# An expert layer's gate matrix with its tokens in pairs, and more of the up products placed beside the routing

## The chip, the cores and the metric

The kernel runs on one NeuronCore of a Trainium2 chip. One launch computes a stack of three model blocks for 256 tokens of width 1024. The metric is the device time of a launch in microseconds (us), as the median of several executions. A profiled execution of the same program gives the busy times, waits and clocks that are quoted here.

The engines are called PE (matrix products; PEld is its loading of the stationary operand), DVE (vector), ACT (scalar and activation), POOL (GpSimd) and SP (which here only issues DMAs). ACT also issues DMAs; both do it in the order of their own queue.

## The reference, cut to what matters

Three blocks follow each other. Only the last layer of the first one is touched by the change. It is a layer of 16384 single-neuron experts: for each token 8 heads pick 16 experts each, through the best sums of two sub-key scores.

```python
def peer_ffn(h, w_q, sub_k1, sub_k2, expert_u, expert_v):
    q = (ht @ w_q).reshape(T, PEER_HEADS, PEER_QDIM)
    s1 = jnp.einsum('thd,nd->thn', q[..., :PEER_HALF], sub_k1)
    s2 = jnp.einsum('thd,nd->thn', q[..., PEER_HALF:], sub_k2)
    v1, i1 = lax.top_k(s1, PEER_TOPK)
    v2, i2 = lax.top_k(s2, PEER_TOPK)
    cand = (v1[..., :, None] + v2[..., None, :]).reshape(T, PEER_HEADS, PEER_TOPK * PEER_TOPK)
    cand_idx = (i1[..., :, None] * PEER_NKEYS + i2[..., None, :]).reshape(...)
    vals, pos = lax.top_k(cand, PEER_TOPK)
    experts = jnp.take_along_axis(cand_idx, pos, axis=-1)
    gates = jax.nn.softmax(vals, axis=-1)
    ...
    u = expert_u[ec]                      # [c, heads, 16, D] of the picked experts
    a = jnp.einsum('cd,chkd->chk', xc, u)
    w = jax.nn.gelu(a) * gc
    return jnp.einsum('chk,chkd->cd', w, expert_v[ec])
```

Here T = 256 tokens, 128 keys on each side, 16 of the best on each side and 16 of the best sums.

## The kernel before

**Streams and products.** All weights come from device memory in chunks of 1 MB, `[128, 2048]` float32. `stream` (line 89) loads a chunk through SP's DMA queue into one of 3 raw buffers and splits it in two halves: ACT casts the high part (L99), and DVE or, if `pool` is set, POOL subtracts it to get the low part (L101). The split parts have 3 buffers in this layer. A float32 product is then three products of the parts (`mm3`, L117 to L119). An *up chunk* holds the up weights of 256 experts; its two halves make 2 x 8 x 3 = 48 matmuls of 256 columns.

**The layer.** The kernel doesn't gather experts. It computes every expert's up product with every token, multiplies it by a dense gate matrix that is zero for experts that were not picked, and multiplies the result by every expert's down weights. There are 64 up chunks and 64 down chunks.

- `routing` (line 791) makes the gate matrix in 48 steps. Steps 0 to 3: query projection, scores against the keys (L804) and the top 16 of both sides on DVE. Steps 4 to 9 and 10 to 15, for the two token tiles: top 16 of the sums, the picked positions back to key indices (L859 to L865, on DVE), and three transposes on PE (L867 twice, L871), so that the indices `iT` and the gates `gT` (high and low float16 parts) lie with the picks on partitions and the tokens along the row. Steps 16 to 47: eight tokens a step. DVE compares the 8 tokens' indices with all 128 keys, which gives the one-hot tiles E (L888) and B (L889), and multiplies E by the two parts of the gates to get A (L892, two instructions). For each token two matmuls (L897) of B and A sum over the picks and give its 128 x 128 gates. ACT takes them out of PSUM, 4 tokens at a time (L900), and after every 16 tokens a 1 MB tile `gt` goes to the device array `gd` (L902).
- `up` (line 904) yields after each up chunk: stream, two products, and GELU on ACT (L912) into a tile `ga`.
- `down` (line 916) runs over the 64 down chunks. Every four chunks it reads 1 MB of gates back (`G`, L936, on ACT's queue). Each chunk multiplies its two `ga` tiles by the gates on DVE (L945), splits them (L112 on ACT, L113 on DVE) and makes 24 matmuls of 512 columns (L928, L929, L931) into four accumulators.

**What sets the order.** `weave` (line 339) emits, after step i of `routing`, n(i) steps of `up`: none before step 7, one a step from 7 to 19, then two of five steps, 24 in all. The first down step emits 5 more up chunks, and each later one emits one, until all 64 are done. The 58 `ga` tiles, one for each half chunk, hold 29 chunks. POOL does the subtractions of the first 29 up chunks, DVE those of the later ones and of all down chunks. Each engine works its queue in order. The tile framework orders the queues by the order of emission, where an engine's operands are ready by its own reckoning, and puts in the waits. The one-hot tiles have 8 buffers, which is two steps of B, E and two A.

In a one-hot tile `[128, 128, 8]` the token is the innermost index, so the 128 columns of one token, which PE reads for L897 as stationary and as moving operand, are 8 float16 apart.

Of the kernel before, what the change touches and what calls it, by code (L numbers as in the profile page):

```python
# [7 lines left out]
F32 = mybir.dt.float32  # L8
# [18 lines left out]
class Core:  # L27
    """Pools and the pieces that every block uses.

    Weights stream through SBUF in chunks of [128, 2048]; each float32 chunk is split  # L30
    exactly into a part with 12 significant bits and the rest, and a float32 product is
    hi*hi + hi*lo + lo*hi, accumulated in float32.
    """
# [18 lines left out]
    def ring(self, ctx, n):  # L52
        """Buffers of the weight stream, n of the split parts."""
        self.raw = ctx.enter_context(self.tc.tile_pool(name="raw", bufs=3))
        self.slots, self.turn, self.early = [], 0, []
        self.more(ctx, n)

    def more(self, ctx, n):
        """n more buffers of the split parts while ctx is open."""
        pool = ctx.enter_context(self.tc.tile_pool(name=f"split{len(self.slots)}", bufs=n))  # L60
        self.slots += [pool] * n

        def less():
            del self.slots[-n:]
        ctx.callback(less)

    def work(self, ctx, half_rows=1):
        """Buffers of the norms: rows of gains, a token tile's rows."""
# [3 lines left out]
    def temp(self, ctx, name):  # L72
        """Buffers of one part of the kernel."""
# [47 lines left out]
    def row(self, name, n=D, src=None, pool=None, tag=None, p=128):  # L121
        """A row of a parameter on every partition."""
# [5 lines left out]
    def rsqrt_n(self, ss, n, m, p=128):  # L128
        """(ss / n + EPS) ** -0.5 for [p, m]."""
# [7 lines left out]
    def rstd(self, parts, n, p=128):  # L137
        """Reciprocal root mean square of rows of n that come in one or two parts [p, m <= 512]."""
# [17 lines left out]
    def pre_norm(self, t, g):  # L156
        """xh, xl[:, :, t] = split(transpose(rmsnorm(X[t]) * g))"""
# [10 lines left out]
    def put_off(self, f, *args):  # L168
        """Emits f(*args), now or at the next flush."""
# [10 lines left out]
    def post_norm(self, t, acc, g, scale, gn=None):  # L180
        """X[t] += scale * rmsnorm(acc) * g, and the next part's pre_norm if it has gains gn."""
# [10 lines left out]
    def residual(self, t, acc, gn):  # L192
        """X[t] += acc, and the next part's pre_norm."""
# [5 lines left out]
    def to_T(self, xn, hi, lo, t, nb, kb0=0, scale=None):  # L199
        """hi, lo[:, kb0.., t] = split(transpose(xn) * scale), scale a power of two."""  # L200
# [15 lines left out]
    def cols_steps(self, w, done):  # L216
        """w: [groups, 2, 128, 4 * N], N <= 512 output columns a group; done(j, t, psum).
        The first two groups go one token tile at a time, as the tiles get ready, if the ring has room."""
# [24 lines left out]
    def linear_stat(self, hl, i, ps):  # L243
        """ps [128, n] = 128 output features by tokens; hl: a chunk [128, 2, 8, 128], i: which half."""
# [5 lines left out]
    def lead(self, ch, done):  # L250
        """Products of the chunks ch one token tile at a time, as the tiles get ready, with the tokens as
        rows; done(c, t, psum [128, 2, 128])."""
# [9 lines left out]
    def pair(self, hl, between=lambda: None):  # L262
        """The two products of a chunk."""
# [6 lines left out]
    def stat_pairs(self, chunk, n, lead=0, row=None):  # L270
        """The two products of each of n chunks. The first chunks go one token tile at a time, with the
        tokens as rows [128, 256] in row(c, t), and are then transposed."""
# [30 lines left out]
    def linear_rows(self, w, hi, lo, done, tail=3, pool=0):  # L303
        """w: [K / 256, 128, 2048] rows in pairs of blocks; hi, lo: [128, K / 128, S]."""
# [34 lines left out]
def weave(main, side, n):  # L339
    """Emits the steps of main, and n[i] steps of side after step i."""  # L340
# [5 lines left out]
def head_norm(k, pool, ps, nh, gain, tag, p=128):  # L346
    """Per-head rmsnorm of ps [p, nh * 64]; returns [p, nh, 64] in SBUF."""
# [13 lines left out]
def rope(k, pool, q, nh, cs, sn, p=128):  # L361
    """Rotary embedding of the first 16 dims of q [p, nh, 64], in place; cs, sn: [p, 16]."""
# [10 lines left out]
def attend(k, pool, p, q, segs, v, identb, sink=None):  # L373
    """Masked attention of p queries and 8 heads.

    q(h): [64, p]; segs(h): (keys [64, n], n, additive mask [p, n] or None) for each piece of the
    keys; v(s, h): [n, 64]. Returns psum [p, 8, 64] before the division, and the factors [p, 8].
    """
# [65 lines left out]
def gelu_small(k, pool, out, x, n, p):  # L444
    """tanh form of gelu for small SBUF tiles, in the table of exp."""
# [10 lines left out]
class Block1:  # L456
# [108 lines left out]
    def compress(self):  # L565
        """The compressed keys and values; yields where the tensor engine would wait."""
# [59 lines left out]
    def cmp_scores(self, t):  # L626
        """Exponentials of the compressed keys' scores [128, 8, 15] and their factors [128, 8]."""
# [21 lines left out]
    def cmp_out(self, s):  # L649
        """psum [128, 8, 64]: the exponentials' products with the compressed values."""  # L650
# [12 lines left out]
    def attention(self, t):  # L663
# [10 lines left out]
        def add(b, o, r, first=False):  # L674
            """y = or += the gated output of branch b"""
# [20 lines left out]
    def flush(self, keep=0):  # L696
        """Emits the transposes that were put off, but for the last."""
# [3 lines left out]
    def merge(self):  # L701
        k, nc, pool = self.k, self.k.nc, self.pool
        M = [k.xn() for t in range(2)]
        for h in range(2):
            ch = [k.stream(k.a["w_up_" + n][h, 0]) for n in "ab"]
            for t in range(2):
                ts = slice(t * 128, t * 128 + 128)
                c = slice(h * 512, h * 512 + 512)
                for i, n in enumerate("ab"):
# [6 lines left out]
                    # sigmoid(z) = (1 + tanh(z / 2)) / 2; the half is in to_T  # L716
# [38 lines left out]
class Peer:  # L755
    """Every expert's product with every token; a gate matrix, zero where the expert was not
    retrieved, weighs them. The gates come from the top-k of the sub-keys' scores; as two float16 parts
    of SCALE times them they keep float32's 24 bits."""

    AHEAD = 58  # L760
# [3 lines left out]
    def __init__(self, k, pool):  # L764
        self.k, self.pool = k, pool
        self.ga = {}
        self.gd = k.dram.tile([128, S // self.GRP, 128, self.GRP], F32, name="gd")

    def consts(self):
        k = self.k  # L770
        tl = lambda n, sh, dt=F32: self.rp.tile(sh, dt, name=n)
        self.iota = tl("iota", [128, 128, 8], F16)
        k.nc.gpsimd.iota(self.iota, pattern=[[1, 128], [0, 8]], base=0, channel_multiplier=0,
# [17 lines left out]
    def routing(self):  # L791
# [21 lines left out]
        for t in range(2):  # L813
# [40 lines left out]
            for j in range(2):  # L854
# [5 lines left out]
                                        self.iota[:, 0:16, None, :].to_broadcast([128, 16, 16, 8]), op=OP.is_equal)  # L860
# [950 lines left out]
```

## Time and profile before

| | us |
|---|---|
| median of 3 runs | 3044.96 |
| lowest and highest of them | 3044.13, 3054.55 |
| the profiled execution, from its first to its last instruction | 3048.1 |
| PE busy in it | 2919.3 |
| the expert layer's steps 4 to 15, with up products | 364 to 463.7 |
| one-hot steps, with up products | 463.7 to 683.3 |
| down chunks with an up chunk each | about 700 to 1090 |
| down chunks alone | about 1090 to 1240 |

How to read what follows. The page of the profile gives each engine's busy time and share of the span, and rows of 40 equal slices (76.2 us each), in which a digit is tenths; PEclk is the clock that PE was granted, in tenths of full speed. A row of the groups names line, engine, operation, tile and shape, then the busy time and the mean duration in ns, then the idle time before them with what ended it. A row of the stages gives the window and its length, the busy time of each engine with its number of instructions, the granted clock, the share of the DMA engines and the GB/s. A row of the waits says who waited for whom: us in total, times, longest. A row of the timeline gives start and duration in us. Matmuls overlap, and their ends are modelled, so starts say more than durations.

### The profile page before, as it was taken

Reading aid. Unit: us, or ns where it says so; the run is one execution under the profiler, and the core shown is the slowest. Engines: PE = TensorE matmul, PEld = TensorE weight load, DVE = VectorE, ACT = ScalarE, POOL = GpSimd, SP = SyncE. Lnnn points to the kernel's source line nnn. Section 1 sums busy time; section 2 is a strip of 40 time slices with the busy share of each in tenths; the row PEclk is TensorE's granted clock in tenths of the full one; section 3 lists DMA queues with packets and bytes.
Section 4 is the critical chain, followed back from the end, with each engine's and each line's share of the span. In section 5 each row is a group of like instructions: output and inputs, shape, how many; then the busy total and the mean of one; then the engine's idle time right before and its main releaser. Section 6 shows DMA issues by size and latency. Waiting matters only on the chain. (4 is left out here: it accounts for less than half of the span.)

```text
span 3048.1 us, 44684 instructions
## 1 busy us (share of the span) xinstructions
PE 2919.3 (96%) x18182; PEld 2586.9 (85%) x18182; DVE 1773.9 (58%) x2984; ACT 1367.2 (45%) x2318; POOL 421.3 (14%) x337
## 2 busy tenths in 40 slices
PE   8999979999999999999679999999999989999999
PEld 6787978889999988898669989898997878878897
DVE  6645693437555555655966555476655555455654
ACT  4533433335444555544535444343544444444543
POOL 2000663221000000000650000032001010000100
PEclk9968988789999999999889999999999899998999
DMA  5512433339766555554325555543554424443453
GB/s 211 187 56 85 153 124 130 134 137 324 251 205 211 206 193 193 205 187 169 131 69 182 185 194 181 192 156 116 175 182 153 145 87 166 152 139 111 145 187 111
DMA packets 105982, 496.74 MB, mean 163 GB/s; under 512 B 11040, under 2 KB 44320, under 8 KB 50224
## 3 DMA queue, kind: packets, MB, share of 16 engines
q1 hardware_dynamic: 61632, 443.15, 42.1%
q10 hardware_dynamic: 44144, 50.74, 5.0%
q8 instruction: 142, 2.33, 0.3%
q14 instruction: 64, 0.52, 0.1%
HBM read 476.03 MB, written 17.83 MB: 162 GB/s over the span
## 5 line engine op out<-in xcount | busy, mean ns | idle before, releaser
L101 DVE TENSOR_TENSOR wl<-raw,wh 128x1024 fp32r<-128x1024 f32 x764 | 915.4, 1219 | 617.7 <-ACT wh L99 616.4
L99 ACT CAST wh<-raw 128x1024 fp32r<-128x1024 f32 x848 | 861.3, 1041 | 708.2 <-PE acc L118 220.5
L117 PE MATMUL tp<-xx,wh 128*128 128x256 f32 (+1 forms) x1440 | 424.2, 295 | 5.6 <-ACT ga L912 5.6
L119 PE MATMUL acc<-xx,wl 128*128 128x256 f32 x1504 | 425.1, 283 | 2.2 <-POOL wl L101 1.4
L117 PE MATMUL acc<-xx,wh 128*128 128x256 f32 x1504 | 424.6, 282 | 2.4 <-DVE hp L1093 2.4
L118 PE MATMUL acc<-xx,wh 128*128 128x256 f32 x1504 | 425.5, 283 | 0.0
L118 PE MATMUL tp<-xx,wh 128*128 128x256 f32 (+1 forms) x1440 | 421.8, 293 | 0.0
L119 PE MATMUL tp<-xx,wl 128*128 128x256 f32 (+1 forms) x1440 | 420.6, 292 | 0.8 <-POOL wl L101 0.8
L117 PEld LDWEIGHTS tp<-xx,wh 128*128 128x128 f32 x1440 | 286.7, 199 | 10.5 <-ACT ga L912 6.0
L118 PEld LDWEIGHTS tp<-xx,wh 128*128 128x128 f32 x1440 | 287.1, 199 | 3.7
L119 PEld LDWEIGHTS acc<-xx,wl 128*128 128x128 f32 x1504 | 286.9, 191 | 2.6 <-POOL wl L101 1.6
L117 PEld LDWEIGHTS acc<-xx,wh 128*128 128x128 f32 x1504 | 286.6, 191 | 2.6 <-issue 2.6
L119 PEld LDWEIGHTS tp<-xx,wl 128*128 128x128 f32 x1440 | 286.4, 199 | 1.8 <-POOL wl L101 1.0
L118 PEld LDWEIGHTS acc<-xx,wh 128*128 128x128 f32 x1504 | 284.7, 189 | 0.0
L147 POOL TENSOR_SCALAR va<-ss 128x1 f32<-128x1 f32 (+1 forms) x49 | 26.0, 531 | 1810.3 <-ACT junk L143 1628.8
L101 POOL TENSOR_TENSOR wl<-raw,wh 128x1024 fp32r<-128x1024 f32 x84 | 219.5, 2630 | 232.8 <-ACT wh L99 221.3
L117 PE MATMUL acc<-wh,xx 128*128 128x256 f32 (+2 forms) x672 | 223.3, 334 | 3.2 <-ACT xx L112 3.2
L118 PE MATMUL acc<-wl,xx 128*128 128x256 f32 (+2 forms) x672 | 219.7, 328 | 4.2 <-DVE wl L101 4.2
L119 PE MATMUL acc<-wh,xx 128*128 128x256 f32 (+2 forms) x672 | 218.7, 328 | 1.2 <-DVE xx L113 1.2
L928 PE MATMUL o<-wh,wth 128*128 128x512 f32 x512 | 200.6, 392 | 0.0
L929 PE MATMUL o<-wl,wth 128*128 128x512 f32 x512 | 200.1, 391 | 0.0
L931 PE MATMUL o<-wh,wtl 128*128 128x512 f32 x512 | 159.9, 391 | 0.0
(480 smaller groups left out, 5113.2 us busy)
## 6 DMA issues: line engine op xcount, KB each, us to landing
raw<-in_ffn_in_dram SPq DMA_DIRECT2D x88, 1024.0 KB, 4.9
raw<-in_peer_u_dram SPq DMA_DIRECT2D x64, 1024.0 KB, 4.9
raw<-in_peer_v_dram SPq DMA_DIRECT2D x64, 1024.0 KB, 4.9
raw<-in_ffn_out_dram SPq DMA_DIRECT2D x44, 1024.0 KB, 4.9
raw<-in_w_up_dram SPq DMA_DIRECT2D x32, 1024.0 KB, 4.9
raw<-in_w_down_dram SPq DMA_DIRECT2D x32, 1024.0 KB, 4.9
gd<-gt ACTq DMA_DIRECT2D x16, 1024.0 KB, 4.0
G<-gd ACTq DMA_DIRECT2D x16, 1024.0 KB, 7.0
```

The lines of the kernel that those rows point to most:

```text
L99: nc.scalar.copy(h[:, c], r[:, c])
L101: eng.tensor_tensor(l[:, c], r[:, c], h[:, c].bitcast(F32), op=OP.subtract)
L117: mm(out, ah, bh, start=start, stop=False)
L118: mm(out, ah, bl, start=False, stop=False)
L119: mm(out, al, bh, start=False, stop=stop)
L147: nc.gpsimd.tensor_scalar(v, ss[:, 0:1], EPS, ss[:, 1:2], op0=OP.add, op1=OP.add)
L928: mm(acc[t][h], wh, vh[:, h], start=st, stop=False)
L929: mm(acc[t][h], wh, vl[:, h], start=False, stop=False)
L931: mm(acc[t][h], wl, vh[:, h], start=False, stop=sp)
```

## The change

It has two parts.

In the one-hot tiles the 8 tokens of a step are laid out as 4 pairs: `[128, 4, 128, 2]`, pair, key, token of the pair. The 128 columns of a token are then 2 float16 apart. The compared table of key numbers is made in that layout, with two columns a key (`iota2`), and the older table keeps only the 16 rows that the index step uses.

The up products are kept by whole chunks in 29 tiles of `[128, 2, 256]`, as much memory as before. During routing 40 chunks are meant to be emitted instead of 24: n(i) is two or one in steps 7 to 19 and then two of three steps. All 40 are split on POOL. Chunks 0 to 21 keep their tile. Chunks 22 to 39 (18 of them) are written to a device array `gs` by a DMA on ACT's queue, and give their tile back. `down` fetches them again, also on ACT's queue, whenever fewer than 27 chunks are held after a chunk was used.

```diff
-    AHEAD = 58
+    SLOTS = 29
+    KEPT = 22
+    AHEAD = 40
...
+        self.held, self.spilled = 0, []
+        self.gs = k.dram.tile([128, self.AHEAD - self.KEPT, 2, S], F32, name="gs")
...
-        self.iota = tl("iota", [128, 128, 8], F16)
-        k.nc.gpsimd.iota(self.iota, pattern=[[1, 128], [0, 8]], base=0, channel_multiplier=0,
+        self.iota = tl("iota", [128, 16, 8], F16)
+        k.nc.gpsimd.iota(self.iota, pattern=[[1, 16], [0, 8]], base=0, channel_multiplier=0,
+                         allow_small_or_imprecise_dtypes=True)
+        self.iota2 = tl("iota2", [128, 128, 2], F16)
+        k.nc.gpsimd.iota(self.iota2, pattern=[[1, 128], [0, 2]], base=0, channel_multiplier=0,
...
-                    oh = lambda n_: pool.tile([128, 128, 8], F16, tag="oh", name=n_, bufs=8)
+                    oh = lambda n_: pool.tile([128, 4, 128, 2], F16, tag="oh", name=n_, bufs=8)
                     B, E = oh("B"), oh("E")
-                    bc = lambda x: x[:, None, c].to_broadcast([128, 128, 8])
-                    nc.vector.tensor_tensor(E, bc(self.iT[0]), self.iota, op=OP.is_equal)
-                    nc.vector.tensor_tensor(B, bc(self.iT[1]), self.iota, op=OP.is_equal)
+                    bc = lambda x: x[:, c].rearrange("p (a b) -> p a b", b=2)[:, :, None].to_broadcast([128, 4, 128, 2])
+                    iota = self.iota2[:, None].to_broadcast([128, 4, 128, 2])
+                    nc.vector.tensor_tensor(E, bc(self.iT[0]), iota, op=OP.is_equal)
+                    nc.vector.tensor_tensor(B, bc(self.iT[1]), iota, op=OP.is_equal)
...
-                                nc.tensor.matmul(ps[:, i, :], B[:, :, z * 4 + i], A[j][:, :, z * 4 + i],
+                                nc.tensor.matmul(ps[:, i, :], B[:, z * 2 + i // 2, :, i % 2], A[j][:, z * 2 + i // 2, :, i % 2],
...
-            hl = k.stream(k.a["peer_u"][c], pool=c < self.AHEAD // 2)
+            hl = k.stream(k.a["peer_u"][c], pool=c < self.AHEAD)
+            g = self.slot()
             for i in range(2):
                 ps = k.tp((128, S), tag="tq")
                 k.linear_stat(hl, i, ps)
-                g = self.pool.tile([128, S], F32, tag="ga", name="ga", bufs=self.AHEAD)
-                nc.scalar.activation(g, ps, AF.Gelu_apprx_tanh)
-                self.ga[c * 2 + i] = g
+                nc.scalar.activation(g[:, i], ps, AF.Gelu_apprx_tanh)
+            if self.KEPT <= c < self.AHEAD:
+                nc.scalar.dma_start(self.gs[:, c - self.KEPT], g)
+                self.spilled.append(c)
+            else:
+                self.ga[c] = g
+                self.held += 1
             yield
+    def slot(self):
+        return self.pool.tile([128, 2, S], F32, tag="ga", name="ga", bufs=self.SLOTS)
+    def fetch(self):
+        while self.spilled and self.held < self.SLOTS - 2:
+            c = self.spilled.pop(0)
+            self.ga[c] = self.slot()
+            self.held += 1
+            self.k.nc.scalar.dma_start(self.ga[c], self.gs[:, c - self.KEPT])
...
-                w = self.ga.pop(e)
+                w = self.ga[c][:, i]
...
+            del self.ga[c]
+            self.held -= 1
+            self.fetch()
...
-            x = i >= 7 if i < 20 else i % 5 in (0, 3)
-            x = min(x, self.AHEAD // 2 - 5 - done[0])
+            x = 0 if i < 7 else 1 + i % 2 if i < 20 else i % 3 > 0
+            x = min(x, self.AHEAD - done[0])
```

The rest of the diff empties lines that held comments.

More of the change, by code (lines that the diff above doesn't have):

```diff
@@ L859, in routing @@
                 nc.vector.tensor_tensor(eq, sel[j].rearrange("p (k h) -> p k h", h=8)[:, None].to_broadcast([128, 16, 16, 8]),
-                                        self.iota[:, 0:16, None, :].to_broadcast([128, 16, 16, 8]), op=OP.is_equal)
+                                        self.iota[:, :, None, :].to_broadcast([128, 16, 16, 8]), op=OP.is_equal)
                 nc.vector.tensor_tensor(eq, eq, ib[:, :, None, :].to_broadcast([128, 16, 16, 8]), op=OP.mult)
```

## The prediction

> **What bounds the kernel now.** I read the page first, then the busy times by stage, and inside the routing stage the groups, the instruction timeline and the waits. The page gives the size of the whole and says which engine to watch.
>
> ```profile
> span 3048.1 us, 44684 instructions
> PE 2919.3 (96%) x18182; PEld 2586.9 (85%) x18182; DVE 1773.9 (58%) x2984; ACT 1367.2 (45%) x2318; POOL 421.3 (14%) x337
> PEclk9968988789999999999889999999999899998999
> ```
>
> PE is busy 96% of the span, so time goes only where PE gets less work, a better clock, or less idle time. Slices 7 to 9 (457 to 686 us) have a granted clock of 0.8, 0.7 and 0.8: that is the expert layer's gate matrix. The stage view cuts that layer at its seams (columns: window, length, then PE, PEld, DVE, ACT and POOL busy, clock, DMA share, GB/s):
>
> ```profile
> 364.00:463.70 99.70, 81.52 (x638) 80.56 (x636) 88.95 (x278) 42.73 (x68) 68.65 (x26) 0.91 0.41 138
> 463.70:683.30 219.60, 219.60 (x1151) 176.55 (x1151) 81.42 (x119) 70.57 (x115) 62.90 (x25) 0.82 0.35 130
> 700.00:1090.00 390.00, 390.00 (x2527) 355.95 (x2526) 236.74 (x342) 191.47 (x285) 0.00 (x0) 1.00 0.70 236
> 1090.00:1240.00 150.00, 150.00 (x667) 124.34 (x666) 84.20 (x108) 77.08 (x109) 0.00 (x0) 1.00 0.57 196
> ```
>
> Row by row: the top-k chain (call it A; PE idle 18.2 us), the one-hot products woven with up products (B; PE always busy, clock 0.82), down products with one up chunk each, down products alone. Only A has idle PE to fill; the last two rows are PE-bound at full clock. So the first question is what B's PE time is made of.
>
> ```profile
> L897 PE MATMUL tp<-A,B 128*128 128x128 f16 x512 | 126.5, 415 | 0.0
> L101 POOL TENSOR_TENSOR wl<-raw,wh 128x1024 fp32r<-128x1024 f32 x25 | 65.0, 2601 | 155.4 <-ACT wh L99 144.2 <-PE tp L897 11.3
> ```
> ```profile
> 477.79 3.93 PE L897 MATMUL tp<-A,B 128*128 128x128 f16 x16
> 481.35 0.48 PE L118 MATMUL tp<-xx,wh 128*128 128x256 f32 x1
> 481.67 0.28 PE L119 MATMUL tp<-xx,wl 128*128 128x256 f32 x1
> ...
> 482.14 0.31 PE L117 MATMUL tp<-xx,wh 128*128 128x256 f32 x1
> ...
> 483.32 0.41 PE L117 MATMUL tp<-xx,wh 128*128 128x256 f32 x1
> ...
> 484.60 0.41 PE L117 MATMUL tp<-xx,wh 128*128 128x256 f32 x1
> ```
>
> Durations overlap on PE, so I take start-to-start times. Four up products take 482.14 - 481.67, 0.1175 us each; an up chunk has 48, 5.64 us. Behind a burst of one-hots six of them take 484.60 - 483.32, 0.213 us each: half clock. The 16 one-hots take 481.35 - 477.79 = 3.56 us, 0.2225 each, although they stream half as many columns. B has 1151 - 512 = 639 other matmuls, 639 x 0.1175 = 75.1 us. The remaining 144.5 us belongs to the 512 one-hots: 512 x 0.2225 = 113.9 us of their own and 30.6 us of lowered clock that comes with them.
>
> ```profile
> DVE A L892 <- PE tp L897: 124.1, 29, 8.5
> ```
>
> DVE waits 124.1 us in B for PE to give back one-hot tiles, so nothing in front of PE is late there.
>
> **The change part by part.**
>
> *One-hots in pairs.* Instruction counts stay: 4 on DVE, 16 on PE and 2 on ACT a step, 32 steps. What changes is the distance between the columns that PE reads, from 8 float16 (16 bytes) to 2 (4 bytes), in both operands. The trace has no one-hot at 4 bytes. The nearest row with 128 columns, dense operands and a new stationary matrix each time is the key product just before A:
>
> ```profile
> 362.89 1.05 PE L804 MATMUL tp<-keys,qpT 128*128 128x128 f32 x8
> 363.70 0.36 PE L117 MATMUL tp<-xx,wh 128*128 128x256 f32 x1
> ```
>
> That is 0.81 / 8 = 0.101 us. The low end is 0.059, half of the 256-column product's 0.1175; the high end is that 0.1175 itself. I take 0.101, the row with the same shape: 512 x 0.101 = 51.7 us (30 to 60). PE that isn't held up by its reads should keep the clock, as in the two last stages, so the 30.6 us goes too. Term: 144.5 - 51.7 = 92.8 us less PE time (84 to 114).
>
> [...]
>
> On DVE the innermost run shrinks from 8 elements to 2. The work stays 1024 elements, and I cost it at nothing: 0.60 us start to start as below. That it falls to the unpacked rate is a rival. The smaller iota tables are made on GpSimd under the query products: nothing.
>
> *More up chunks during routing.* The weave gives 20 chunks in steps 7 to 19 (7 odd steps with 2, 6 even with 1) and 19 in steps 20 to 47, so 39; the 40th comes with the first down step. Before, 24. The chunks themselves cost the same wherever they stand: moved, not removed. They help only where PE was idle, and cost where they make a new wait. All 40 are now split on GpSimd (29 before), and DVE shares something with it:
>
> ```profile
> 548.52 2.41 POOL L101 TENSOR_TENSOR wl<-raw,wh 128x1024 fp32r<-128x1024 f32 x1 [1.58 <-ACT wh L99]
> 548.61 2.87 DVE L889 TENSOR_TENSOR B<-iT,iota 128x1024 f16<-128x1024 f16 x1
> ...
> 553.50 0.69 DVE L888 TENSOR_TENSOR E<-iT,iota 128x1024 f16<-128x1024 f16 x1
> 554.10 0.68 DVE L889 TENSOR_TENSOR B<-iT,iota 128x1024 f16<-128x1024 f16 x1
> ```
>
> A DVE compare that starts just behind a GpSimd subtraction ends 0.55 us after it: it waited the whole of it, then ran. So I count the two as one resource. In B, PE needs: A did 638 matmuls, about 13 chunks, which leaves 26 of the 39: 26 x 5.64 + 51.7 = 198 us. DVE and GpSimd together need 52 x 2.41 + 32 x 4 x 0.60 = 125 + 77 = 202 us. Before it was 25 x 2.41 + 77 = 137 of 219.6, with room; now the pair is as late as PE. Hand-overs cost between nothing and what the 25 subtractions of B show over an undisturbed one, 2.60 - 2.41 = 0.19 us, times 52 = 10 us. I take 5: B lasts 207 us, PE idles 9 of them. Queued behind a late subtraction is the next one on GpSimd; who waits is PE, for the chunk's low part. Behind a late compare stand the three others of its step; who waits is PE for A and B, with one step of tiles in hand.
>
> [...]
>
> In A I leave PE's 18.2 us of idle time as it is. It is caused by transposes that stand in PE's queue before their DVE input is there:
>
> ```profile
> PE tp L867 <- DVE idx L865: 12.5, 2, 7.5
> PEld tp L867 <- issue: 7.7, 1, 7.7
> ```
>
> Ends: 18 us better if the extra chunks fill it, 24 us worse if 5 more chunks (14 instead of 9 are handed out by step 15), 10 subtractions of 2.41 us, all push DVE's chain back.
>
> *Put aside and fetched.* 18 writes and 18 reads of 256 KB, all on ACT's queue. The nearest rows are four times as large:
>
> ```profile
> gd<-gt ACTq DMA_DIRECT2D x16, 1024.0 KB, 4.0
> G<-gd ACTq DMA_DIRECT2D x16, 1024.0 KB, 7.0
> L902 ACTq DMA_DIRECT2D gd<-gt x16: 326/326/340, 477.8 to 683.8; - x16
> ```
>
> Issuing 36 costs ACT 36 x 0.33 = 12 us, half of them in B, where ACT is busy 70.6 of 219.6 us, and half in the down stage, where it is busy 77 of 150. A fetch is issued three chunks ahead. A down chunk has 24 matmuls:
>
> ```profile
> 1179.72 0.39 PE L928 MATMUL o<-wh,wth 128*128 128x512 f32 x1
> ...
> 1180.63 0.39 PE L928 MATMUL o<-wh,wth 128*128 128x512 f32 x1
> ```
>
> Four take 0.91 us, so a chunk takes 5.46 and the lead is 16 us, against 7.0 us for the larger read. Two tiles of the 29 are free when a fetch asks, so its issue shouldn't hold ACT. Cost nothing while that lead holds; without it, the fourth rival. DMA is at a share of 0.57 there and the reads add 5 MB in 100 us, about 50 GB/s to 196.
>
> *The seam.* At the first down step DVE waits long for the gate matrix to come back:
>
> ```profile
> DVE ga L945 <- DMA G<-gd: 32.8, 5, 24.5
> ```
>
> PE is covered by five up chunks (28 us), before and after. Four of them are now split on DVE, which is idle in that wait. Nothing.
>
> *Sum.* 92.8 less PE time, 9 us new idle time in B: 84 us. The profiled execution spans 3048.1 us, which would become 2964; its span is 3.1 us above the median of the three runs, so from the median 3044.96 - 84 = 2961 us. The end of B comes near 463.7 + 207 = 671 us instead of 683, with 39 chunks done instead of 26.
>
> **The rivals.**
>
> 1. *Hand-overs fail.* DVE and GpSimd don't overlap with PE's one-hots: one step of tiles in hand is too little, since four compares queued behind four subtractions take 4 x 2.87 = 11.5 us. Then each of 32 steps takes 202 / 32 = 6.3 us of the pair plus 16 x 0.101 = 1.6 us of PE, 253 us in all, 55 idle. Gain 92.8 - 55 = 38: 3007 us. For it: A, where both engines are pressed, leaves PE 18% idle. Against: three split buffers let GpSimd run ahead. [...]
>
> 2. *Pairs cost DVE its packed rate.* Then a compare takes what a 128x1024 float32 subtraction takes:
>
> ```profile
> L101 DVE TENSOR_TENSOR wl<-raw,wh 128x1024 fp32r<-128x1024 f32 x197 | 235.2, 1222 | 127.5 <-ACT wh L99 127.5
> ```
>
> The pair needs 125 + 128 x 1.22 = 281 us, PE idles 83, gain 10: 3035 us. The pairs are still adjacent float16, which is against it.
>
> 3. *The distance isn't the reason, so the first part doesn't do what it is made for.* A dense bfloat16 product among the attention's small ones also starts 0.22 us before the next:
>
> ```profile
> 226.74 0.29 PE L396 MATMUL tp<-cmask,identb 128*128 128x128 bf16 x1
> 226.96 0.79 PE L394 MATMUL tp<-kT,qTb 64*128 64x128 f32 x2
> ```
>
> There the clock was 0.6 and the forms alternate, which is against it. One-hots would stay at 144.5, PE would need 291 us in B and hide the pair: 3045 us.
>
> 4. *Slower: the fetches come in series.* If a fetch waits on ACT's queue for a tile that the chunk just used gives back, the casts behind it wait too, and each of 18 fetches is paid in full: 18 x 7.0 = 126 us, against 84 gained: 42 slower, 3087 us. It decides from 84 / 18 = 4.7 us a fetch on. For it: the 24.5 us wait above shows what a transfer in the chain costs. Against: the lead of 16 us.
>
> **How the numbers follow.** A measurement of this kernel can tell about 0.5% (15 us) from no change. Forecast 0.83, at 2961 us; rivals 0.07, 0.03, 0.03, 0.04. The forecast's own ends: PE term 84 to 114, A from +18 to -24, B's idle 4 to 14. All good ends together give 128 (2917), all bad ones 46 (2999); the range 2925 to 3003 leaves off a little of the first and reaches nearly to rival 1. Faster by over 0.5%: 0.83 + 0.07 = 0.90; within: rivals 2 and 3, 0.06; slower: 0.04.
>
> **What would show it.** Right: L897 starts about 0.1 us apart and its group is no longer PE's heaviest in routing; the clock in B is near 1.0; the first down products start near 690 us; down products alone last some 43 chunks x 5.46 = 235 us instead of 150, with PE full. New waits of PE for GpSimd's low parts, or of PE for A, sum to about 9 us in B. Wrong: compares at 1.2 us (rival 2), one-hots still at 0.22 (rival 3), PE gaps in every step (rival 1), gaps between chunks 21 and 40 of the down stage with ACT held at an issue (rival 4).

## The result, and the profile after

The changed kernel takes 2957.24 us (median of 4 runs, 2954.26 to 2962.95), beside 3046.05 us for the kernel before on the same chip (4 runs, 3044.13 to 3054.55). The ratio is 0.9704, with a 95% interval of 0.9685 to 0.9723: 88.8 us faster. Line numbers move by 7 to 25: the compares are now L897 and L898, A is L901, the one-hot matmuls L906, GELU L921, the fetch L939, the gates' multiplication L970 and the down matmuls L953 to L956.

From the page of the profile after: span, busy times, granted clock by slices.

```profile
span 2955.6 us, 44739 instructions
PE 2806.4 (95%) x18182; PEld 2514.9 (85%) x18182; DVE 1812.5 (61%) x2962; ACT 1361.3 (46%) x2318; POOL 485.4 (16%) x360
PEclk9978989999999999999889999999999999998999
```

PE has the same 18182 matmuls and is busy for 112.9 us less. Slices 7 to 9, at 0.8, 0.7 and 0.8 before, are at 0.9. The span fell by 92.5 us: the layer's last down product ends 87.5 us earlier (1165.8 us, 1253.3 before), and the other 5.0 us lie behind the layer, where the change touches nothing.

The stages of the layer after, cut at the first one-hot, the last one-hot, and, for the down products, where the up products run out (columns as before: window, length, PE, PEld, DVE, ACT, POOL busy, clock, DMA share, GB/s):

```profile
364.00:503.20 139.20, 117.95 (x949) 117.32 (x948) 92.27 (x271) 57.87 (x90) 94.83 (x39) 0.91 0.42 144
503.20:666.40 163.20, 154.01 (x1494) 150.58 (x1493) 148.30 (x122) 87.70 (x145) 107.55 (x37) 0.97 0.71 253
666.40:906.00 239.60, 238.09 (x1592) 219.27 (x1591) 133.49 (x175) 117.60 (x178) 0.00 (x0) 1.00 0.68 231
906.00:1165.80 259.80, 251.43 (x1088) 206.22 (x1087) 170.33 (x276) 127.83 (x188) 1.63 (x2) 0.98 0.72 241
```

Stage A is longer by 39.5 us, as it holds 949 matmuls instead of 638. B shrinks from 219.6 to 163.2 us with 343 more other products in it; its clock is 0.97 instead of 0.82; and PE, always busy there before, now idles 9.2 us. In the last row, down products alone, PE idles 8.4 us, 2.4 of them at the very end, as before; from 1090 to 1240 us of the kernel before, down products alone too, it was always busy.

Since chunks move between the stages, lengths alone mislead. So I use one account for all kernels. From the length of a stage I take what its ordinary products need at their undisturbed start-to-start times: 0.1175 us for each up matmul (48 a chunk) and 0.2275 us for each down matmul (0.91 / 4). What is left is the stage's *excess*: idle time, lowered clock, and the one-hots themselves. A runs from 364 us to the first one-hot, B to the last one-hot, D to the last down product. A and B stand for these stages; where the one-hot tiles of the same names are meant, the text says tile A and tile B.

| excess, us (PE idle of it) | A | B | D | sum |
|---|---|---|---|---|
| before | 26.5 (18.2) | 144.6 (0) | 7.8 (3.2) | 178.9 |
| after | 28.5 (21.2) | 47.8 (9.2) | 16.7 (9.9) | 93.0 |
| pairs_only | 27.0 (19.2) | 53.6 (14.4) | 6.2 (3.2) | 86.8 |
| forty_only | 28.5 | 150.8 (0) | 17.4 (11.5) | 196.7 |
| quads | 28.0 | 61.0 (0) | 16.2 | 105.2 |
| dense | 30.3 | 102.2 (52.2) | 16.3 | 148.8 |
| a_pairs | 28.3 | 48.5 (7.5) | 16.4 | 93.2 |
| b_pairs | 28.3 | 144.9 (0) | 16.3 | 189.5 |
| dve_late | 28.2 | 33.2 (0) | 14.9 (8.7) | 76.3 |
| spread | 28.2 | 44.7 (7.4) | 3.1 (2.5) | 76.0 |
| both | 28.5 | 33.2 (0) | 4.0 | 65.7 |
| pairs_dve | 28.5 | 36.6 (2.1) | 8.7 | 73.8 |
| both_all | 8.8 (4.4) | 33.1 (0) | 3.2 | 45.1 |
| spread_twice | 28.7 | 44.7 | 10.5 (7.8) | 83.9 |

The fall of the sum from before to after, 85.9 us, is the change inside the layer; with the 16 up matmuls that now lie ahead of 364 us (1.9 us) it makes 87.8, within 0.3 of the 87.5. B gives 96.8, A takes back 2.0 and D 8.9.

The timeline of B after, one burst of one-hots and the up product behind it:

```profile
503.16 1.09 PE L906 MATMUL tp<-A,B 128*128 128x128 f16 x16
504.06 0.36 PE L117 MATMUL tp<-xx,wh 128*128 128x256 f32 x1
```

Sixteen one-hots take 0.90 us instead of 3.56: 0.056 each, 28.8 us for all 512. The groups in B (busy us, mean ns, idle before and who ended it):

```profile
L101 POOL TENSOR_TENSOR wl<-raw,wh 128x1024 fp32r<-128x1024 f32 x37 | 109.7, 2985 | 38.1 <-ACT wh L99 37.9
L901 DVE TENSOR_TENSOR A<-E,gT 128x1024 f16<-128x1024 f16 x60 | 73.2, 1258 | 16.3 <-PE tp L906 16.3
L897 DVE TENSOR_TENSOR E<-iT,iota 128x1024 f16<-128x1024 f16 x29 | 43.9, 1514 | 0.0
L906 PE MATMUL tp<-A,B 128*128 128x128 f16 x512 | 39.6, 227 | 9.2 <-DVE A L901 8.7 <-ACT gt L909 0.5
```

DVE waited 124.1 us for PE to give tiles back before, and waits 16.3 now; PE waits 8.7 us for DVE's tile A. The bound has changed sides. That the means of DVE are 1258 and 1514 ns doesn't say that pairs are slow, as the row of L901 (it makes tile A) with its minimum and median shows (duration min/median/max in ns):

```profile
L901 DVE TENSOR_TENSOR A<-E,gT x64: 674/680/2903, 442.0 to 659.6; 128x1024 f16<-128x1024 f16 x64
```

An undisturbed one takes 680 ns, as before. The rest of the mean is time spent behind a subtraction on POOL: without those in B the mean is 685 ns (dve_late, below). 37 subtractions of 2.41 us and some 120 DVE instructions of 0.60 us are 161 of B's 163.2 us, and by the trace one or the other of the two engines is busy in 155.5 of them: the pair of DVE and POOL is the bound.

B's clock of 0.97 goes with PE's waits. The granted clock in it is 1.00 but for three stretches of 3.4 us at 0.5, from 558.0, 612.7 and 640.0 us. Each begins within 0.7 us of the end of one of PE's three longest waits there (1.5 us to 557.6, 2.4 to 613.2, 2.5 to 640.6).

### The profile page after: what moved, and what is told of

Its sections match the earlier page's. It is cut to its first block, busy times and chain, and to the rows that moved or that the text cites. A ratio compares the mean times of both kernels' runs of the same rounds, so it can differ in the third digit from the quotient of the medians.

```text
span 2955.6 us, 44739 instructions
## 1 busy us (share of the span) xinstructions
PE 2806.4 (95%) x18182; PEld 2514.9 (85%) x18182; DVE 1812.5 (61%) x2962; ACT 1361.3 (46%) x2318; POOL 485.4 (16%) x360
## 5 line engine op out<-in xcount | busy, mean ns | idle before, releaser
L101 DVE TENSOR_TENSOR wl<-raw,wh 128x1024 fp32r<-128x1024 f32 (+1 forms) x742 | 887.5, 1218 | 568.0 <-ACT wh L99 567.0
L117 PE MATMUL tp<-xx,wh 128*128 128x256 f32 (+1 forms) x1440 | 412.5, 286 | 14.0 <-ACT ga L921 14.0
L119 PE MATMUL tp<-xx,wl 128*128 128x256 f32 (+1 forms) x1440 | 409.6, 284 | 0.0
L118 PE MATMUL tp<-xx,wh 128*128 128x256 f32 (+1 forms) x1440 | 409.6, 284 | 0.0
L101 POOL TENSOR_TENSOR wl<-raw,wh 128x1024 fp32r<-128x1024 f32 x106 | 284.1, 2703 | 123.2 <-ACT wh L99 123.0
L117 PEld LDWEIGHTS tp<-xx,wh 128*128 128x128 f32 x1440 | 275.1, 191 | 16.9 <-ACT ga L921 14.4
L118 PEld LDWEIGHTS tp<-xx,wh 128*128 128x128 f32 x1440 | 275.0, 191 | 1.8
L119 PEld LDWEIGHTS tp<-xx,wl 128*128 128x128 f32 x1440 | 275.0, 191 | 0.0
L953 PE MATMUL o<-wh,wth 128*128 128x512 f32 x512 | 201.7, 394 | 0.0
L956 PE MATMUL o<-wh,wtl 128*128 128x512 f32 x512 | 161.1, 393 | 0.9 <-DVE wtl L113 0.9
```

The costliest lines, as they stand in the source:

```text
L101: eng.tensor_tensor(l[:, c], r[:, c], h[:, c].bitcast(F32), op=OP.subtract)
L117: mm(out, ah, bh, start=start, stop=False)
L118: mm(out, ah, bl, start=False, stop=False)
L119: mm(out, al, bh, start=False, stop=stop)
L953: mm(acc[t][h], wh, vh[:, h], start=st, stop=False)
L956: mm(acc[t][h], wl, vh[:, h], start=False, stop=sp)
```

## The experiments

Theory: nearly all of the gain is that PE no longer reads one-hot columns 16 bytes apart; the 40 chunks add nothing. Rival: the chunks carry part of it, or it is not the distance. Later runs ask what holds B now, and what D lost.

### Each part alone

**pairs_only** is the kernel before with the one-hot tiles of the change and nothing else of it:

```diff
-oh = lambda n_: pool.tile([128, 128, 8], F16, tag="oh", name=n_, bufs=8)
+oh = lambda n_: pool.tile([128, 4, 128, 2], F16, tag="oh", name=n_, bufs=8)
...
-nc.tensor.matmul(ps[:, i, :], B[:, :, z * 4 + i], A[j][:, :, z * 4 + i],
+nc.tensor.matmul(ps[:, i, :], B[:, z * 2 + i // 2, :, i % 2], A[j][:, z * 2 + i // 2, :, i % 2],
```

> The kernel before with the pair layout alone (24 chunks in routing, nothing put aside). Theory (PE's reads 16 bytes apart were the cost): a one-hot matmul takes 0.056 us as in the changed kernel, 28.7 us for 512; B then needs 75 us of other products + 29 = 104 us of PE, but 25 GpSimd subtractions and 128 compares need 25 x 2.41 + 77 = 137 us, so PE idles about 33 us in B, clock near 1.0: gain about 144.5 - 137 + 75 = 82 us, 2964 us. Rival (the chunks moved into routing carry the gain): within 20 us of the kernel before.

**forty_only** is the changed kernel with the one-hot tiles of before:

```diff
-oh = lambda n_: pool.tile([128, 4, 128, 2], F16, tag="oh", name=n_, bufs=8)
+oh = lambda n_: pool.tile([128, 128, 8], F16, tag="oh", name=n_, bufs=8)
...
-nc.tensor.matmul(ps[:, i, :], B[:, z * 2 + i // 2, :, i % 2], A[j][:, z * 2 + i // 2, :, i % 2],
+nc.tensor.matmul(ps[:, i, :], B[:, :, z * 4 + i], A[j][:, :, z * 4 + i],
```

> The changed kernel with its one-hot tiles in the old layout. Theory: PE has no idle time in the one-hot stage to fill, the stage only gets longer by 13 chunks; the fetches cost the down stage about 9 us as they do in the changed kernel: 5 to 12 us slower than before, 3051 to 3058 us. Rival (the moved chunks carry the gain): at least 20 us faster than before.

pairs_only takes 2955.76 us, a ratio of 0.969 (0.9673 to 0.9708) to the kernel before, which had 3049.46 us on that chip. forty_only takes 3068.81 us, 1.0062 (1.0044 to 1.008). Their stage B, each in turn:

```profile
463.80:592.50 128.70, 114.32 (x1151) 110.74 (x1149) 119.58 (x119) 65.87 (x115) 80.52 (x25) 0.95 0.59 221
```
```profile
504.80:770.90 266.10, 266.10 (x1493) 223.38 (x1492) 89.75 (x123) 91.97 (x145) 92.01 (x37) 0.83 0.45 160
```

With pairs alone the same 1151 matmuls take 128.7 instead of 219.6 us. PE idles 14.4 us in it, not the 33 expected, and B is shorter than the 137 us of the pair's count. With the 119 DVE instructions of the row that count is 25 x 2.41 + 119 x 0.60 = 132 us, so it comes out a few us too high.

With 40 chunks alone the clock stays at 0.83 and PE is always busy; the longer B holds more up products at that clock. The kernel is 19.4 us slower than the one before (0.6%, the interval lies above 1), more than the 5 to 12 us expected: the excess grows by 9.6 us in D, as expected, but also by 6.2 in B and 2.0 in A, which wasn't. The chunks by themselves make the kernel slower; the whole gain is the layout's. The rival falls.

### The distance

**quads** lays out two groups of four tokens, so that columns are 8 bytes apart, and **dense** one token after the other, 2 bytes:

```diff
-oh = lambda n_: pool.tile([128, 4, 128, 2], F16, tag="oh", name=n_, bufs=8)
+oh = lambda n_: pool.tile([128, 2, 128, 4], F16, tag="oh", name=n_, bufs=8)
...
```

> The changed kernel with groups of four tokens, columns 8 bytes apart. [...]

```diff
-oh = lambda n_: pool.tile([128, 4, 128, 2], F16, tag="oh", name=n_, bufs=8)
+oh = lambda n_: pool.tile([128, 8, 128], F16, tag="oh", name=n_, bufs=8)
...
+bc = lambda x: x[:, c][:, :, None].to_broadcast([128, 8, 128])
...
```

> The changed kernel with each token's 128 columns side by side (2 bytes apart). [...] DVE: the compared value is then constant along the innermost run, and I expect the unpacked rate, 1.1 to 1.2 us a compare instead of 0.68; DVE and GpSimd then need 37 x 2.41 + 120 x 1.13 = 225 us in the one-hot stage where they needed 161: 50 to 65 us slower than the changed kernel, about 3015 us. If the stage is bound by PE and not by that pair: within 10 us of the changed kernel.

One run each: quads 2975.53 us, dense 3018.79 us. The timeline of a burst and the product behind it, and B as a whole, for quads:

```profile
511.81 2.05 PE L906 MATMUL tp<-A,B 128*128 128x128 f16 x16
513.61 0.37 PE L117 MATMUL tp<-xx,wh 128*128 128x256 f32 x1
```
```profile
504.20:680.60 176.40, 176.40 (x1494) 173.86 (x1493) 140.15 (x123) 90.71 (x145) 97.13 (x37) 1.00 0.68 240
```

and the burst for dense:

```profile
515.70 1.09 PE L906 MATMUL tp<-A,B 128*128 128x128 f16 x16
516.60 0.36 PE L118 MATMUL tp<-xx,wh 128*128 128x256 f32 x1
```

Start to start, 16 one-hots take 0.90 us at 2 bytes, 0.90 at 4, 1.80 at 8 and 3.56 at 16: from 4 bytes on the time grows in proportion to the distance. At 8 bytes PE runs at a clock of 1.00 and is never idle, and its excess of 61.0 us is almost only the one-hots' own 512 x 0.1125 = 57.6.

Whether columns 8 bytes apart would cost what 4 bytes cost (0.056 us a one-hot) or half of what 16 cost (0.11) was open before the run. It is the second, 0.1125: for PE's reads here, 8 bytes already cost double.

dense loses its time elsewhere. PE's reads are as fast as in pairs, yet PE idles 52.2 us of B. The row of tile A's instruction in dense, below B's, says why:

```profile
507.10:724.70 217.60, 165.44 (x1494) 160.24 (x1493) 200.98 (x121) 88.19 (x145) 149.41 (x37) 0.88 0.51 187
```
```profile
L901 DVE TENSOR_TENSOR A<-E,gT x64: 1210/1214/3439, 446.5 to 721.6; 128x1024 f16<-128x1024 f16 x64
```

With one token's value repeated along the whole innermost run, DVE takes 1214 ns instead of 680 for the same 1024 elements. That is the loss that the second rival of the prediction feared for pairs: it is real, and pairs escape it.

**a_pairs** keeps the stationary tile B at 16 bytes and puts only the moving tile A (and E) in pairs, **b_pairs** the reverse. The lines that make the tiles change with it:

```diff
-B[:, z * 2 + i // 2, :, i % 2], A[j][:, z * 2 + i // 2, :, i % 2],
+B[:, :, z * 4 + i], A[j][:, z * 2 + i // 2, :, i % 2],
...
```

> The changed kernel with only E and A, the moving operand, in pairs; B in the old layout. If the moving operand's reads are the cost: near 0.06 to 0.1 us a one-hot. If the stationary operand's loading is: 0.15 us or more.

```diff
-B[:, z * 2 + i // 2, :, i % 2], A[j][:, z * 2 + i // 2, :, i % 2],
+B[:, z * 2 + i // 2, :, i % 2], A[j][:, :, z * 4 + i],
...
```

> The changed kernel with only B, the stationary operand, in pairs; E and A in the old layout. If the moving operand's reads are the cost: 0.15 us or more a one-hot, clock below 0.9 in the stage. If the stationary operand's loading is: near 0.06. If each costs by itself: about 0.13 to 0.15.

One run each: a_pairs 2959.96 us, b_pairs 3061.06 us. Their bursts:

```profile
508.06 1.17 PE L908 MATMUL tp<-A,B 128*128 128x128 f16 x16
509.04 0.37 PE L118 MATMUL tp<-xx,wh 128*128 128x256 f32 x1
```
```profile
508.49 3.82 PE L908 MATMUL tp<-A,B 128*128 128x128 f16 x16
511.94 0.57 PE L117 MATMUL tp<-xx,wh 128*128 128x256 f32 x1
```

a_pairs has 0.98 us, b_pairs 3.45 us, with a lowered clock (0.83 over b_pairs' B, 0.98 over a_pairs'). So nearly all of it is the moving operand's distance. The stationary one at 16 bytes costs 0.08 us in 16 here, and 0.13 and 0.14 in the next two whole bursts (1.03 and 1.04 us, from 513.98 and 520.77 us).

### What holds B now

**dve_late** gives POOL the subtractions of the first 20 chunks only, about those of stage A, and DVE the rest. If B is held by the exclusion of the two engines, it goes although DVE has more to do:

```diff
-pool=c < self.AHEAD)
+pool=c < 20)
```

> The changed kernel with up chunks 20 to 39 split by DVE instead of GpSimd, so that nothing runs on GpSimd in the one-hot stage. Theory (DVE and GpSimd exclude each other and bound that stage at 161 of 164 us): DVE alone needs 120 x 0.60 + 37 x 1.22 = 117 us, PE 116 + 29 = 145, so the stage falls by 10 to 18 us and compares wait no more: 2940 to 2948 us. Rival (DVE's queue order is the limit, not the shared resource): no gain, or slower, since subtractions now stand behind compares that wait for tiles.

It takes 2949.76 us, 0.9666 (0.965 to 0.9682), 2 us above the range expected. Stage B, and the group that makes tile A:

```profile
504.30:652.80 148.50, 148.50 (x1493) 146.49 (x1493) 118.27 (x158) 87.47 (x145) 0.00 (x0) 1.00 0.77 276
```
```profile
L901 DVE TENSOR_TENSOR A<-E,gT 128x1024 f16<-128x1024 f16 x60 | 38.7, 685 | 14.8 <-PE tp L906 14.8
```

DVE has 36 more instructions in B and is busy 30 us less; tile A's instruction takes 685 ns in the mean instead of 1258. PE is never idle, the clock is 1.00, and B is 14.7 us shorter. The subtraction takes 2.41 us of the shared pair on POOL, 1.22 us on DVE. What remains of B's excess, 33.2 us, is the one-hots' 28.8 and little else. B is bound by PE again.

### What D lost

**spread** emits an up chunk at every second down step instead of at each, so that up products last until the fetches are done:

```diff
-for _ in range(1 if c else 5):
+for _ in range(c % 2 if c else 5):
```

> The changed kernel with the remaining up chunks at every second down step (to step 39) instead of every one (to step 20), so that the fetches start at step 2 and run far ahead. Theory (the fetches come too late, three chunks ahead, in the first down chunks alone): PE's gaps between 940 and 1020 us go, 8 to 11 us less: 2946 to 2950 us. Rival (the gaps are from the load on DMA, not from the lead): same total load, within 4 us of the changed kernel.

It takes 2948.77 us, 0.9668 (0.9652 to 0.9684), and D as a whole is

```profile
664.40:1150.20 485.80, 483.26 (x2678) 422.31 (x2677) 303.53 (x450) 245.57 (x364) 1.62 (x2) 1.00 0.71 242
```

with an excess of 3.1 us instead of 16.7. What the changed kernel does without that cover is seen in its own timeline, ACT's queue first and then DVE in the same stretch (in brackets: idle time before, and who ended it; L113 is the subtraction that reads a `ga` tile for the last time):

```profile
930.97 0.33 ACTq L939 DMA_DIRECT2D ga<-gs  x1
931.34 0.41 ACT L112 CAST wth<-ga 128x256 fp32r<-128x256 f32 x1 [1.65 <-DVE wtl L113]
933.91 0.33 ACTq L939 DMA_DIRECT2D ga<-gs  x1
934.34 0.41 ACT L112 CAST wth<-ga 128x256 fp32r<-128x256 f32 x1 [2.59 <-DVE wtl L113]
...
942.33 0.33 ACTq L939 DMA_DIRECT2D ga<-gs  x1
942.75 0.41 ACT L112 CAST wth<-ga 128x256 fp32r<-128x256 f32 x1 [5.80 <-DVE ga L970]
...
981.61 0.33 ACTq L939 DMA_DIRECT2D ga<-gs  x1
```
```profile
933.47 0.42 DVE L113 TENSOR_TENSOR wtl<-ga,wth 128x256 fp32r<-128x256 f32 x1
935.84 0.76 DVE L970 TENSOR_TENSOR ga<-ga,G 128x256 f32<-128x256 f32 x2 [1.96 <-DMA ga<-gs]
...
939.27 0.42 DVE L970 TENSOR_TENSOR ga<-ga,G 128x256 f32<-128x256 f32 x1 [2.33 <-DMA ga<-gs]
...
941.88 0.42 DVE L113 TENSOR_TENSOR wtl<-ga,wth 128x256 fp32r<-128x256 f32 x1
...
947.57 0.76 DVE L970 TENSOR_TENSOR ga<-ga,G 128x256 f32<-128x256 f32 x2 [0.73 <-DMA ga<-gs]
```

Each wait of DVE ends 4.9 to 5.4 us behind an issue of a fetch (930.97 to 935.84, 933.91 to 939.27, 942.33 to 947.57), which is the fetch's landing time (median 5.2 us in this profile). So the lead is one landing, not three chunks. The issue in its turn waits for DVE: those at 933.91 and 942.33 come 0.02 and 0.03 us behind the ends of L113, and so do all from 915.52 on. Most likely the fetch waits for the tile that L113 gives back; that it is the tile was not tried by itself. ACT, which issues the fetches in its queue, stands still meanwhile (2.59 and 5.80 us): a ring of fetch, multiplication, subtraction, next fetch.

From 930.97 to the last fetch at 994.01 the ring takes 63.04 us for 10 chunks, 6.30 each, while PE needs 5.46. PE feels it late, through subtractions that stand in DVE's queue behind the waiting multiplications. Its waits from 900 us to the end of the fetches, and two rows of the stages:

```profile
PE o L954 <- DVE wl L101: 5.1, 2, 2.8
PE o L956 <- DVE wtl L113: 0.9, 2, 0.5
```
```profile
980.00:1000.00 20.00, 18.30 (x72) 14.37 (x72) 12.35 (x26) 7.45 (x12) 0.00 (x0) 0.91 0.66 224
1000.00:1020.00 20.00, 18.40 (x74) 15.09 (x75) 20.00 (x42) 8.72 (x14) 0.00 (x0) 0.91 1.08 334
```

That is 6.0 us of idle time between 955 and 1002 us, and 0.09 x 40 = 3.6 us of lowered clock behind it, which is about D's 8.9. In spread DVE still waits 30.2 us for fetches (32.1 in the changed kernel), but the late ones are issued 16.57 us apart (7 from 864.71 to 964.11), with two down chunks and an up chunk for PE in between, and none of them comes behind an L113. The ring is gone: six of these seven come with the GELU of an up chunk, as here:

```profile
864.70 0.38 ACT L921 ACTIVATE ga<-tp 128x256 f32<-128x256 f32 x1 [0.84 <-PE tp L119]
864.71 0.33 ACTq L939 DMA_DIRECT2D ga<-gs  x1
```

**spread_twice** makes each fetch of spread two identical ones, to double their load with the same lead:

```diff
 self.k.nc.scalar.dma_start(self.ga[c], self.gs[:, c - self.KEPT])
+self.k.nc.scalar.dma_start(self.ga[c], self.gs[:, c - self.KEPT])
```

> The spread run with every fetch issued twice into the same tile, 36 reads of 256 KB. If PE's gaps in the down stage came from too short a lead: no gaps come back, excess of the down stage within 3 us of the 3.1 us of spread. If they came from the load on DMA: 5 us or more of them come back.

One run, 2952.22 us; D's excess is 10.5 us. The row of the fetches' first lines:

```profile
L939 ACTq DMA_DIRECT2D ga<-gs x18: 326/327/7257, 688.4 to 970.4; - x18
```

One issue held ACT's queue for up to 7.26 us, most likely since the second read into a tile waits for the first. So this run doubled the time in the queue together with the bytes, and doesn't tell load from lead. It is inconclusive. That the late issue and not the load on DMA costs the time in D is read from the waits and not tried by itself.

### Better versions

**both** joins dve_late and spread. **both_all** is spread with no subtraction on POOL at all (`pool=c < 0`). **pairs_dve** is pairs_only, thus without the 40 chunks and their DMAs, with POOL's subtractions for the first 13 chunks only (`pool=c < 13`).

> The changed kernel with up chunks 20 to 39 split by DVE and the remaining up chunks at every second down step, both as in the runs before. If the two costs are separate they add: the one-hot stage at 149 us as with the first, the down stage without gaps as with the second; from the profiles 14.6 + 13.6 = 28 us less than the changed kernel, ratio to the kernel before about 0.961. If the second only moved the first one's waiting: no better than either alone, 0.966.

> The kernel before with the pair layout and GpSimd's subtractions only for up chunks 0 to 12: nothing put aside, 24 chunks in routing. If the moved chunks are not needed at all: the one-hot stage needs 75 + 29 = 104 us of PE and 77 + 25 x 1.22 = 107 us of DVE, so 107 to 112 us instead of 128.7; 17 to 21 us less than the pair layout alone, ratio about 0.963, within 4 us of the run named both. If the moved chunks help once DVE and GpSimd no longer exclude each other: at least 8 us slower than both.

> As the run named both, but all 40 up chunks are split by DVE, so that nothing runs on GpSimd beside the top-k chain either. If PE's 21 us of idle time before the one-hots come from that exclusion: 8 to 15 us less than both. If they come from the length of DVE's own chain (some 45 us of it, now with 39 x 1.22 = 48 us of subtractions in the same queue): the same or up to 20 us slower.

| | median us | ratio to before (95%) |
|---|---|---|
| both | 2934.93 | 0.9637 (0.9624 to 0.965) |
| pairs_dve | 2938.57 | 0.9646 (0.9632 to 0.9659) |
| both_all | 2920.58 | 0.9582 (0.9566 to 0.9597) |

The gains of dve_late and spread add up: 33.2 and 4.0 us of excess in B and D. The ratio expected for both, 0.961, lies just below the measured interval. pairs_dve comes to within the intervals of both with none of the chunk machinery (its profiled execution was the longest of its runs, so its excess is if anything too high). B of pairs_dve:

```profile
465.30:574.50 109.20, 107.08 (x1130) 105.00 (x1129) 98.24 (x141) 64.18 (x113) 0.00 (x0) 0.98 0.71 259
```

both_all is the fastest kernel, 36.7 us below the changed one by medians of different chips, 125.8 below the kernel before on its own, and 14.4 below both. What it adds over both lies in A, the first row; the second is B:

```profile
364.00:484.70 120.70, 116.29 (x958) 115.78 (x956) 103.32 (x317) 59.05 (x91) 0.00 (x0) 0.97 0.51 176
484.70:633.20 148.50, 148.50 (x1494) 146.46 (x1493) 118.25 (x158) 87.41 (x145) 0.00 (x0) 1.00 0.77 276
```

PE idles 4.4 us in A, in the changed kernel 21.2. What it waited for there, and what ACT waited for at the same time:

```profile
PE tp L117 <- ACT ga L921: 14.0, 2, 11.3
PE tp L874 <- DVE idx L872: 7.2, 1, 7.2
```
```profile
ACT g L836 <- DVE g L835: 14.1, 2, 11.3
```

The GELU (L921) stands in ACT's queue behind the exponential of the gates (L836), which waits for DVE, and the transpose (L874) waits for DVE too. So both go back to DVE's top-k chain. In both_all ACT waits only 1.8 us for L835. The heaviest step of that chain in A, the changed kernel first and then both_all:

```profile
L866 DVE TENSOR_TENSOR eq<-xb,iota 128x2048 f16<-128x2048 f16 x4 | 9.3, 2323 | 0.0
```
```profile
L866 DVE TENSOR_TENSOR eq<-xb,iota 128x2048 f16<-128x2048 f16 x4 | 4.9, 1216 | 0.0
```

Next to POOL's subtractions it takes 2323 ns, without them 1216. DVE's work in A is 92.3 us in the changed kernel; in both_all it is 103.3 with 39 subtractions, which take 47.1, so 56.2 without them. The order of DVE's queue is another one too in both_all, and the run doesn't separate the two.

## Why the prediction was right, and where it was not

The result, 2957.24 us, is 3.8 us below the forecast and for the main reason given. But the closeness is luck in part: B gave 13.0 us more than forecast, A and D took 10.9.

- **One-hots.** Mechanism right, term mis-sized. That columns 4 bytes apart would cost what neighbouring ones cost was my estimate, and it holds: 0.90 us for 16 in pairs and in dense. I took 0.101 us from a row of the same shape with float32 operands; it was 0.056, even below the low end of 0.059. That is 512 x 0.045 = 23 us more gain. Among the rows that I read there was no float16 product with neighbouring columns at full clock.
- **The lowered clock.** Right in kind: from 0.82 to 0.97. Not all of the 30.6 us goes: B's excess of 47.8 is 28.8 of one-hots, 9.2 idle and 9.8 left over. A clock of 0.97 explains about half of that (0.03 x 163.2 = 4.9 us), and it goes with PE's waits. The other half is there in dve_late too, where PE is never idle and the clock 1.00: 4.4 us are left.
- **B bound by the pair of DVE and POOL, 9 us idle.** 9.2 us measured, and that the two agree is luck, for the counts behind them were off: I left 13 chunks to A, and the weave put 19.6 there, so B had 37 subtractions and not 52 and started 39.5 us later. Both sides of the comparison shrank together (PE 20.5 x 5.64 + 28.8 = 144.4 us, the pair 161), so the difference, which I had put at 4 us and hand-overs, was larger, and the hand-overs cost next to nothing. PE's idle time is less than this difference of 17 us, since part of it is the lowered clock and the leftover above. B's end at 666.4 us (671 forecast) and the first down product at 692 (690) came out right.
- **A, nothing.** 2.0 us longer. The 18 us of idle time could not be filled by more chunks, since the subtractions of those chunks are what slows DVE's chain. I had named that cost as the bad end and missed that it stood in the kernel before already; taking the subtractions away (both_all) gains 19.7 us.
- **Fetches, nothing.** This step failed. "Cost nothing while that lead holds": the lead of 16 us did not hold, and D lost 8.9 us. I counted it in emitted chunks and in PE's time. On the queues it was one landing, 5.2 us. "Two tiles of the 29 are free when a fetch asks, so its issue shouldn't hold ACT" did not hold either: the issues came only behind DVE's L113. This is the fourth rival's mechanism, fetches in series on ACT's queue, but at 0.84 us a chunk instead of 7.0, since most of each fetch was still beside a chunk's matmuls. That is far below the 4.7 us at which the rival would have decided. Down products alone last 259.8 us instead of 235: 1088 matmuls x 0.2275 = 247.5 us, and 12.3 of loss, 4.8 of which lie in the last 66 us and are there before too.
- **Compares, nothing.** Right, 680 ns; the second rival fell. dense shows its loss one step further.
- **The third rival** fell with quads and b_pairs: the distance is the reason, and only that of the moving operand.
- **The second part of the change.** I forecast no gain from it of its own, and it has none: pairs_only is as fast as the whole. I had not forecast that it costs some 18 us of excess beside the old layout (forty_only), half of it in D.

Not tried: both_all's choice of engine with the 24 chunks of before, which the likeness of both and pairs_dve suggests would be about as fast. That the waits lower the clock, and not something that comes with both, is read from the traces alone.

## What to carry to other kernels

When a matmul starts far apart for the columns it streams, look at the distance between the columns of its moving operand; here 2 and 4 bytes cost the same (0.056 us) and 8 bytes twice that, and interleaving just two tokens kept DVE's instruction at 680 ns as well. Moving vector work to POOL is no relief when both engines exclude each other and POOL takes twice the time (here 2.41 us a subtraction against 1.22): count the two as one resource before handing work over. Judge a prefetch by the time from its issue on its own queue to the wait that it ends, not by the number of loop steps between them, ask what the issue itself waits for, and give it other work to hide behind.

## What the runs showed of the hardware that was not expected

- The time of a float16 matmul with 128 columns was 0.056, 0.056, 0.1125 and 0.2225 us with the moving columns 2, 4, 8 and 16 bytes apart. The same distance of 16 bytes in the stationary operand cost 0.005 us (0.061 against 0.056) in the burst shown (0.008 and 0.009 in the next two).
- At 8 bytes the granted clock stayed at 1.00 with PE never idle; at 16 bytes it fell to 0.82 and 0.83, and the products behind a burst started 0.213 us apart instead of 0.1175.
- With the moving columns 2 or 4 bytes apart the clock of B was 1.00, 0.97, 0.95 and 0.88 with 0, 9.2, 14.4 and 52.2 us of PE's idle time (dve_late, the changed kernel, pairs_only, dense). In the changed kernel it was at 0.5 for three stretches of 3.4 us in B, each beginning within 0.7 us of the end of a wait of PE, and for 3.4, 6.8 and 13.6 us in A, beginning just behind or within PE's three longest waits there (2.7, 7.2 and 11.3 us).
- DVE's two-input instruction on 1024 float16 took 680 ns with runs of two elements, and 1214 ns with a value repeated along the innermost run.
